# Seven units with seven products, at every second place, in both halves of the second product of two SwiGLU FFNs (fp32, split into high and low parts)

## The chip, the core and the metric

The kernel runs on one core of a Trainium2 chip. The metric is the device time of one execution in microseconds (us). The engines are TensorE (PE; its weight loads are shown apart as PEld), VectorE (DVE), ScalarE (ACT), GpSimd (POOL) and the queues that issue transfers, of which SyncE's (SP) carries the weights.

## The reference

One layer of a hybrid decoder on x of 256 rows and 2048 columns, in float32: a SwiGLU half step, a merge of two gated linear attentions, and a second SwiGLU half step, each with a norm ahead and behind.

```
def rms_norm(x, w):
    y = x * lax.rsqrt(jnp.mean(x * x, axis=-1, keepdims=True) + EPS)
    return y * w

def swiglu(x, w_gate, w_up, w_down):
    return (jax.nn.silu(x @ w_gate) * (x @ w_up)) @ w_down

f1 = swiglu(rms_norm(h, ffn1_pre_norm), ffn1_w_gate, ffn1_w_up, ffn1_w_down)
h = h + 0.5 * rms_norm(f1, ffn1_post_norm)
m = hybrid_token_mixer(rms_norm(h, mix_pre_norm), ...)
h = h + rms_norm(m, mix_post_norm)
f2 = swiglu(rms_norm(h, ffn2_pre_norm), ffn2_w_gate, ffn2_w_up, ffn2_w_down)
h = h + 0.5 * rms_norm(f2, ffn2_post_norm)
```

w_gate and w_up are 2048 x 5504, w_down is 5504 x 2048. The change concerns the product with w_down, once in each FFN.

## The kernel before

Every product of two fp32 matrices is three matmuls of rounded parts: each operand is split into a high part (hi, a copy by ACT to the rounded type fp32r) and a remainder (lo = x - hi, a subtraction by DVE), and PE adds hi by hi, lo by hi and hi by lo into one PSUM tile (mm3, L159 to L161). Each weight that is read from memory costs ACT a copy and DVE a subtraction; the left operand is split too.

The second product of an FFN (down_proj, L589) has 256 rows (two tiles t of 128), 2048 columns in two halves (hf) of two blocks of 512 each, and 5504 summands in 43 tiles kt of 128. Two neighbouring kt make a unit u; there are 21 units and one tile over. A half keeps four sums c in PSUM (two t by two blocks). In the second half, the last seven kt (DTAIL) are held back and done block by block.

- A plain kt loads 128 x 1024 of weights (raw, L135), splits them (whi by ACT at L153, wlo by DVE at L155) and does four products of three matmuls each: 8 products in a unit.
- A unit with seven products (Blocks.seven, L267) treats its 2 x 2 blocks with Strassen's scheme in Winograd's form. It loads four pieces of 128 x 512 into two raw tiles, makes three sums of the weights (wsum, and one in place in raw), splits the four that it needs and the three sums (whi, wlo and wsumh, wsuml), and does 7 products, three into c and four into p, some of them with sums of the left operand (part "d", "s2", "s3", "s4"). Its products p1, p5, p6, p7 collect in four more PSUM tiles (p) over all units of the half. In the order of the code the products are p1, c01, c00, p6, p5, p7, c10; wsuml is needed first by the third matmul of p5.
- share (L306) folds the four p into sums that close adds to the c at the end of the half. Its additions are named psum.
- The sums of the left operand for one unit (sums_of, L762) are four operations of 128 x 128 on DVE (sums, L205 to L208) and a split of 128 x 512. They are made one unit ahead of their first use.

Which units have seven products is set by two tables: DSUMS (3, 7, 11, 15) in both halves, whose operand sums are made in the first half and kept (the first three in the tiles xhi0, xlo0, xhi1, which are free then; they are called held in the profile; the last in a work tile called sums), and DMORE, (9, 19) in the first half and (5, 13) in the second, whose sums are made for the one use in the tiles of the left operand's parts (hkhi, hklo; 4 buffers each).

The left operand's parts of a unit (hkhi by ACT, hklo by DVE, 128 x 512) are made in each half anew from hT. The ring has five buffers each of raw, whi and wlo; the row tiles (wsum, wsumh, wsuml and the sums' first form) have three buffers together.

The code's order is not the engines' order. A scheduler gives each engine a fixed list by priority and by its own idea of when operands are ready; an engine then works through its list in order, waiting where it must. Four loads of the post norm's weights (load_bcast, L384, on ACT's queue) stand at kt 8 to 11 of the first half.

Of the kernel before, what the change touches and what calls it, by code (L numbers as in the profile page):

```python
# [7 lines left out]
F32 = mybir.dt.float32  # L8
F32R = mybir.dt.float32r
# [23 lines left out]
AHEAD = 3  # L33
SUMS = (2, 4, 6)
FOUR = (2, 4, 5, 6)
DSUMS = (3, 7, 11, 15)
DMORE = ((9, 19), (5, 13))
DTAIL = 7
O_GQ, O_GK, O_GV, O_GO, O_CODE = 0, 512, 1024, 2048, 3072
O_HQ, O_HF, O_HI, O_HO, O_ZG, O_ZH = 3088, 4112, 5136, 6160, 7184, 9232  # L40
# [48 lines left out]
def kernel(ctx: ExitStack, tc: tile.TileContext, a: dict, out: bass.AP):  # L89
# [13 lines left out]
    uid, last, first_ops = [0], [None], []  # L103

    def nm(s):
        uid[0] += 1
        return f"{s}_{uid[0]}"
# [276 lines left out]
    def load_bcast(t, name, n, after):  # L384

        with tc.issue_after(after.ins):
            nc.scalar.dma_start(t, a[name][:, n * CB:(n + 1) * CB].broadcast_to([P, CB]))
# [15 lines left out]
    def tiles4(x):  # L403
        return x.rearrange("p (k c) -> p k c", c=P)
# [47 lines left out]
    def square(src, ss, n):  # L452
        sq = work.tile([P, CB], BF16, tag="sq", name=nm("sq"), bufs=1)
        nc.scalar.activation(sq, src, AF.Square, accum_out=ss[:, n:n + 1])  # L454
# [134 lines left out]
    def down_proj(w_dram, nkt, lhs, sums_of, post, pre, wpost, ys, homes, following):  # L589

        acc = [[None] * 4 for _ in range(NT)]
        nxt, rs, ready = ([None] * NT, [None] * NT, [0] * NT), [None, None], []
        ss = [small.tile([P, 4], F32, tag="ss", name=nm("ss")) for _ in range(NT)]
        parts = {}

        def split(hf, kt, alloc=ring_alloc):
            return wchunk(w_dram[kt * P:(kt + 1) * P, hf * 1024:(hf + 1) * 1024]
                          .rearrange("p (n c) -> p n c", n=2), CB, alloc)  # L600

        def weigh(t, n):
            square(acc[t][n], ss[t], n)
            o = acc[t][n]
            if n < 2:
                o = ys()
            elif at_end(t, n):
                o = tmp()

            nc.vector.tensor_tensor(o, acc[t][n], wpost[n], op=ALU.mult)  # L610
            acc[t][n] = o

        def at_end(t, n):
            return pre is None and (t, n) == (NT - 1, 3)

        def tmp():
            return work.tile([P, CB], F32, tag="tmp", name=nm("y"), bufs=3)

        ahead = []
        for hf in range(2):  # L620
            lhs_h = lhs()
            b = Blocks(lambda i, kt: w_dram[kt * P:(kt + 1) * P,
                                            (2 * hf + i) * CB:(2 * hf + i + 1) * CB],
                       CB, lhs_h, part_of(parts))
            n = nkt - DTAIL if hf else nkt
            units = sorted(DSUMS + DMORE[hf])
            kt = 0
            while kt < n:
                u = kt // 2
                if kt % 2 == 0 and u + 1 in units and u + 1 not in parts:  # L630
                    parts[u + 1] = sums_of(u + 1)
                if u in units:
                    b.seven(u, u == units[-1])
                    kt += 2
                    continue
                chunk = ahead.pop(0) if ahead else split(hf, kt)
                if kt == 2 * units[-1] + 2:
                    ahead = [split(hf, kt + 1)]
                    b.share()
                if not hf and kt in (8, 9, 10, 11):  # L640
                    load_bcast(wpost[kt - 8], post, kt - 8, last[0])
                for t in range(NT):
                    for i in range(2):
                        b.plain((kt,), t, i, chunk[i:i + 1], kt == nkt - 1)
                if not hf and kt == 1:
                    side.flush()
                kt += 1
            if not hf:
                ahead = [split(1, kt) for kt in range(2)]
                for t in range(NT):  # L650
                    for i in range(2):
                        acc[t][i] = b.close(t, i)
                        weigh(t, i)
        tail = []
        for i, kt in enumerate(range(nkt - DTAIL, nkt)):
            tail.append((kt, split(1, kt, homes[i])))

            lhs_h(0, kt)
        for t in range(NT):
            for n in (2, 3):  # L660
                for i, (kt, chunk) in enumerate(tail):
                    b.plain((kt,), t, n - 2, chunk[n - 2:n - 1], kt == nkt - 1)
                    if i % 2:
                        side.pump()
                    if following is not None and t == 0 and i == 3 * (n - 2):
                        ready.append(following(len(ready)))

                acc[t][n] = b.close(t, n - 2, tmp() if at_end(t, n) else None)
                weigh(t, n)
                if following is not None and (t, n) == (0, 2):  # L670
                    ready.append(following(len(ready)))
                side.pump()
            side.spawn(settled(t, acc, ss[t], 0.5, pre, nxt, rs))
        return nxt, rs, ready


    def ffn(pre, x, rs, post, pre_next, begin=None, ready=(), then=None):
        with ExitStack() as fctx:
# [4 lines left out]
            def new_part(i):  # L683
                s = ("hkhi", "hklo")[i]
                return fwork.tile([P, 2, NT * P], F32R, tag=s, name=nm(s), bufs=4)
# [34 lines left out]
            for j, f0 in enumerate(blocks):  # L720
# [3 lines left out]
                if j or begin:  # L724
                    g, u, ready = gemm_pair(
                        [(a[pre + "_w_gate"], f0), (a[pre + "_w_up"], f0)], w, xl, sums, ready,
                        following, () if j else raws, (FOUR if j % 2 else SUMS) if j else ())
# [8 lines left out]
                if not (j or begin):  # L736
                    side.spawn(x_sums())
                    u = gemm_block(a[pre + "_w_up"], f0, w, xl)
# [19 lines left out]
            def in_x(s, dt):  # L758
                return tpool.tile([P, 4, CB], dt, tag=s, name=nm("held"))

            wpost = in_x("xlo1", F32)
            def sums_of(u):  # L762
                v = hT[u // 2][:, u % 2 * 2:u % 2 * 2 + 2, :]
                f = row_tile("sums")[:, 0, :]
                four_sums(v[:, 0, :P], v[:, 1, :P], v[:, 0, P:], v[:, 1, P:],
                          *[f[:, k * P:(k + 1) * P] for k in range(4)])
                if any(u in more for more in DMORE):
                    hi, lo = [new_part(i).rearrange("p i c -> p (i c)") for i in range(2)]
                elif u != DSUMS[-1]:
                    home = in_x(("xhi0", "xlo0", "xhi1")[DSUMS.index(u)], F32R)  # L770
                    hi, lo = home[:, 0, :], home[:, 1, :]
                else:
                    hi, lo = [work.tile([P, CB], F32R, tag="tmp", name=nm("sums"), bufs=3)
                              for _ in range(2)]
                split_into(hi, lo, f)
                return tiles4(hi), tiles4(lo)
# [593 lines left out]
```

## Time and profile before

| | |
|---|---|
| time, median of 3 runs | 2064.32 us (2063.22 to 2066.75) |
| the profiled execution's own time | 2066.25 us |
| its span in the profile | 2064.3 us |
| PE busy | 2051.2 us (99%) |
| DVE busy | 1858.0 us (90%) |
| ACT busy | 1304.9 us (63%) |
| DMA, mean over the span | 205 GB/s |

A row of the timeline has the start, the duration, engine, line, operation, what it writes and reads, and its shape; in square brackets stands how long the engine was idle before it and what ended that. A row "PE p L161 <- DVE wsuml L245: 1.8, 3, 0.7" says that PE's matmuls into p of line 161 waited for DVE's wsuml 1.8 us in all, three times, 0.7 at the longest. Matmuls overlap each other, so their durations add up to more than the time that they take. The second products stand at about 462 to 690 us (FFN1) and 1836 to 2058 us (FFN2).

### The profile page before, as it was taken

How to read it: one execution, taken by the hardware profiler on the slowest of the kernel's cores; microseconds unless marked ns; L12 is line 12 of the kernel's file. 1: busy time of each engine (PE TensorE's matmuls, PEld its weight loads, DVE VectorE, ACT ScalarE, POOL GpSimd, SP SyncE). 2: the span in 40 equal slices, each digit the busy share in tenths (PEclk: the TensorE clock that was granted, in tenths of full speed). 3: DMA queues.
4: the chain of work that ended last, by engine and by line, in shares of the span. 5: the costliest groups of instructions: out<-in, count | busy, mean ns of one | idle time of the engine just before them, and what ended most of it. 6: DMA issues, size and time to landing. Idle time of an engine off the chain costs nothing. (4 is left out here: it accounts for less than half of the span.)

```text
span 2064.3 us, 28994 instructions
## 1 busy us (share of the span) xinstructions
PE 2051.2 (99%) x10337; PEld 1702.9 (82%) x10337; DVE 1858.0 (90%) x2187; ACT 1304.9 (63%) x1714; POOL 41.1 (2%) x87
## 2 busy tenths in 40 slices
PE   9999999999999999999999999999999999999998
PEld 9888888888888888878888888888888888888886
DVE  7999999998999779989999897578999999999996
ACT  7666666666666576577655554465666666766663
POOL 1000000000000100000000000010000000000000
PEclk9999999999999999999999999999999999999999
DMA  8767677676767467556565566747767767776663
GB/s 261 215 208 241 196 220 218 209 227 207 226 196 230 148 198 222 162 174 192 169 203 188 181 223 214 218 157 200 234 193 218 227 210 215 219 235 200 213 206 133
DMA packets 246105, 423.50 MB, mean 205 GB/s; under 512 B 63476, under 2 KB 71863, under 8 KB 245960
## 3 DMA queue, kind: packets, MB, share of 16 engines
q1 hardware_dynamic: 194896, 401.80, 61.7%
q10 hardware_dynamic: 51064, 19.84, 4.8%
q8 instruction: 81, 1.33, 0.3%
q14 instruction: 64, 0.52, 0.1%
HBM read 406.11 MB, written 4.19 MB: 199 GB/s over the span
## 5 line engine op out<-in xcount | busy, mean ns | idle before, releaser
L155 DVE TENSOR_TENSOR wlo<-raw,whi 128x1024 fp32r<-128x1024 f32 (+3 forms) x498 | 582.8, 1184 | 70.9 <-ACT whi L153 70.0
L153 ACT ACTIVATE whi<-raw 128x1024 fp32r<-128x1024 f32 (+3 forms) x498 | 504.8, 1026 | 217.5 <-PE c L160 74.0
L159 PE MATMUL c<-whi,xhi 128*128 128x512 f32 (+1 forms) x1270 | 494.5, 390 | 0.0
L161 PE MATMUL c<-wlo,xhi 128*128 128x512 f32 (+1 forms) x1270 | 491.5, 387 | 0.0
L160 PE MATMUL c<-whi,xlo 128*128 128x512 f32 (+1 forms) x1270 | 491.3, 387 | 0.0
L245 DVE TENSOR_TENSOR wlo<-raw,whi 128x1024 fp32r<-128x1024 f32 x252 | 299.4, 1218 | 36.9 <-ACT whi L284 23.6
L161 PEld LDWEIGHTS c<-wlo,xhi 128*128 128x128 f32 x1270 | 238.4, 188 | 47.9 <-DVE wlo L245 0.8
L159 PEld LDWEIGHTS c<-whi,xhi 128*128 128x128 f32 x1270 | 238.4, 188 | 47.4 <-ACT xhi L471 0.6
L160 PEld LDWEIGHTS c<-whi,xlo 128*128 128x128 f32 x1270 | 238.5, 188 | 46.2
L284 ACT ACTIVATE whi<-raw 128x1024 fp32r<-128x1024 f32 x126 | 133.1, 1057 | 201.2 <-DVE raw L245 95.0
L245 DVE TENSOR_TENSOR wsuml<-wsum,wsumh 128x1536 fp32r<-128x1536 f32 x126 | 220.6, 1751 | 8.0 <-ACT wsumh L286 8.0
L160 PE MATMUL c<-whi,hklo 128*128 128x512 f32 x558 | 217.2, 389 | 0.3 <-DVE hklo L155 0.3
L161 PE MATMUL c<-wlo,hkhi 128*128 128x512 f32 x558 | 217.2, 389 | 0.1
L159 PE MATMUL c<-whi,hkhi 128*128 128x512 f32 x558 | 217.2, 389 | 0.0
L282 ACT ACTIVATE wsumh<-wsum 128x1024 fp32r<-128x1024 f32 x126 | 132.6, 1053 | 92.7 <-DVE wsum L245 70.7
L280 ACT ACTIVATE whi<-raw 128x1024 fp32r<-128x1024 f32 x126 | 132.4, 1051 | 60.8 <-PE c L160 49.4
L245 DVE TENSOR_TENSOR wsum<-raw,raw 128x1024 f32<-128x1024 f32 x126 | 153.4, 1218 | 18.2 <-DMA raw<-in_ffn_w_down_dram 15.7
L160 PEld LDWEIGHTS c<-whi,hklo 128*128 128x128 f32 x558 | 104.7, 188 | 22.3 <-DVE hklo L155 0.6
L161 PEld LDWEIGHTS c<-wlo,hkhi 128*128 128x128 f32 x558 | 104.7, 188 | 22.2 <-DVE wlo L245 0.5
L159 PEld LDWEIGHTS c<-whi,hkhi 128*128 128x128 f32 x558 | 104.7, 188 | 21.8
L245 DVE TENSOR_TENSOR c<-c,psum 128x512 f32<-128x512 f32 x135 | 87.4, 690 | 11.5 <-PE c L161 11.2
L245 DVE TENSOR_TENSOR wsum<-raw 128x512 f32<-128x512 f32 x126 | 87.0, 690 | 3.6
(346 smaller groups left out, 3153.4 us busy)
## 6 DMA issues: line engine op xcount, KB each, us to landing
raw<-in_ffn_w_down_dram SPq DMA_DIRECT2D x124, 512.0 KB, 4.7
raw<-in_w_in_dram SPq DMA_DIRECT2D x104, 512.0 KB, 4.5
raw<-in_ffn_w_gate_dram SPq DMA_DIRECT2D x90, 512.0 KB, 4.6
raw<-in_ffn_w_up_dram SPq DMA_DIRECT2D x90, 512.0 KB, 4.4
raw<-in_ffn_w_gate_dram SPq DMA_DIRECT2D x140, 256.0 KB, 4.0
raw<-in_ffn_w_up_dram SPq DMA_DIRECT2D x140, 256.0 KB, 3.9
raw<-in_w_in_dram SPq DMA_DIRECT2D x128, 256.0 KB, 3.6
raw<-in_ffn_w_down_dram SPq DMA_DIRECT2D x96, 256.0 KB, 3.7
```

The source lines that it names most:

```text
L153: last[0] = nc.scalar.activation(hi, src, AF.Copy)
L155: nc.vector.tensor_tensor(lo, src, hi.bitcast(F32), op=ALU.subtract)
L159: nc.tensor.matmul(ps, lhsT=xhi, rhs=whi, start=start, stop=False)
L160: nc.tensor.matmul(ps, lhsT=xlo, rhs=whi, start=False, stop=False)
L161: nc.tensor.matmul(ps, lhsT=xhi, rhs=wlo, start=False, stop=stop)
L245: return nc.vector.tensor_tensor(o, x, y, op=op)
L280: nc.scalar.activation(ahi, ra, AF.Copy)
L282: nc.scalar.activation(hi[:, 0:2, :], wsum[:, 0:2, :], AF.Copy)
L284: nc.scalar.activation(bhi, rb, AF.Copy)
```

## The change

The units with seven products are 3, 5, 7, 9, 11, 13 and 15 in both halves: seven instead of six in each half, 28 instead of 24 in the two second products. Units 9 and 19 of the first half and 5 and 13 of the second were among them before; now 5, 9 and 13 are in both halves, and 19 in none. The operand sums of all seven are made in the first half and kept: two units' sums share each of xhi0, xlo0 and xhi1, of which only half was used before, and the seventh stays in the work tiles. Sums are made 7 times in an FFN, before 8 times (6 in the first half, 2 in the second). Since kt 10 and 11 are now a unit with seven products, two of the four loads of the post norm's weights stand at kt 12 and 13.

```
-DSUMS = (3, 7, 11, 15)
-DMORE = ((9, 19), (5, 13))
+DSUMS = (3, 5, 7, 9, 11, 13, 15)
...
-            units = sorted(DSUMS + DMORE[hf])
+            units = DSUMS
...
-                if not hf and kt in (8, 9, 10, 11):
-                    load_bcast(wpost[kt - 8], post, kt - 8, last[0])
+                if not hf and kt in (8, 9, 12, 13):
+                    col = (8, 9, 12, 13).index(kt)
+                    load_bcast(wpost[col], post, col, last[0])
...
-            wpost = in_x("xlo1", F32)
+            wpost, homes = in_x("xlo1", F32), []
...
-                if any(u in more for more in DMORE):
-                    hi, lo = [new_part(i).rearrange("p i c -> p (i c)") for i in range(2)]
-                elif u != DSUMS[-1]:
-                    home = in_x(("xhi0", "xlo0", "xhi1")[DSUMS.index(u)], F32R)
-                    hi, lo = home[:, 0, :], home[:, 1, :]
+                i = DSUMS.index(u)
+                if i % 2 == 0 and i < 6:
+                    homes.append(in_x(("xhi0", "xlo0", "xhi1")[i // 2], F32R))
+                if i < 6:
+                    hi, lo = [homes[-1][:, 2 * (i % 2) + k, :] for k in range(2)]
                 else:
```

What it makes of the engines' lists lies within the two second products. The first place is DVE's list in the first half of FFN1, from the remainder of unit 3's sums on (wsuml_4254). Before (raw_4302 and raw_4325 are unit 4, raw_4344 and raw_4367 unit 5, raw_4394 the first tile of unit 6):

```order
L245 TENSOR_TENSOR wsuml_4254<-wsum_4252,wsumh_4253 128x1536
L155 TENSOR_TENSOR wlo_4305<-raw_4302,whi_4304 128x1024
L155 TENSOR_TENSOR hklo_4310<-hT_1661,hkhi_4309 128x512
L155 TENSOR_TENSOR wlo_4328<-raw_4325,whi_4327 128x1024
L155 TENSOR_TENSOR wlo_4347<-raw_4344,whi_4346 128x1024
L205 TENSOR_TENSOR sums_4386<-hT_2008 128x128
L155 TENSOR_TENSOR hklo_4352<-hT_1661,hkhi_4351 128x512
L206 SCALAR_TENSOR_TENSOR sums_4386<-sums_4386,hT_2008 128x128
L155 TENSOR_TENSOR wlo_4370<-raw_4367,whi_4369 128x1024
L207 TENSOR_TENSOR sums_4386<-hT_2008 128x128
L208 TENSOR_TENSOR sums_4386<-hT_2008,sums_4386 128x128
L155 TENSOR_TENSOR wlo_4397<-raw_4394,whi_4396 128x1024
```

Now (raw_4309 and raw_4332 are unit 4, wsum_4353 unit 5; sums_4302 and held_4207 are unit 5's operand sums; line numbers are one lower):

```order
L244 TENSOR_TENSOR wsuml_4254<-wsum_4252,wsumh_4253 128x1536
L154 TENSOR_TENSOR wlo_4312<-raw_4309,whi_4311 128x1024
L204 TENSOR_TENSOR sums_4302<-hT_1661 128x128
L206 TENSOR_TENSOR sums_4302<-hT_1661 128x128
L205 SCALAR_TENSOR_TENSOR sums_4302<-sums_4302,hT_1661 128x128
L154 TENSOR_TENSOR hklo_4317<-hT_1661,hkhi_4316 128x512
L207 TENSOR_TENSOR sums_4302<-hT_1661,sums_4302 128x128
L154 TENSOR_TENSOR wlo_4335<-raw_4332,whi_4334 128x1024
L154 TENSOR_TENSOR hklo_4375<-hT_1661,hkhi_4374 128x512
L154 TENSOR_TENSOR held_4207<-sums_4302,held_4207 128x512
L154 TENSOR_TENSOR hklo_4415<-hT_2008,hkhi_4414 128x512
L244 TENSOR_TENSOR wsum_4353<-raw_4351,raw_4352 128x1024
```

Behind unit 3 stood the weights of three plain units; now one plain unit, the next operand sums and the next unit's weight sums stand there.

The second place is DVE's list behind unit 15 of the same half. Before (wlo_4816 is still unit 15, hklo_4859 is the left operand of unit 16, hklo_4899 of unit 17):

```order
L245 TENSOR_TENSOR wsuml_4808<-wsum_4806,wsumh_4807 128x1536
L245 TENSOR_TENSOR wlo_4816<-raw_4805,whi_4815 128x1024
L155 TENSOR_TENSOR hklo_4859<-hT_3767,hkhi_4858 128x512
L205 TENSOR_TENSOR sums_4932<-hT_4102 128x128
L155 TENSOR_TENSOR wlo_4855<-raw_4852,whi_4854 128x1024
```

Now (wsuml_4836 is unit 15's, wlo_4883, wlo_4889 and hklo_4899 are unit 16's, psum is share):

```order
L244 TENSOR_TENSOR wsuml_4836<-wsum_4834,wsumh_4835 128x1536
L154 TENSOR_TENSOR wlo_4883<-raw_4880,whi_4882 128x1024
L154 TENSOR_TENSOR wlo_4889<-raw_4886,whi_4888 128x1024
L244 TENSOR_TENSOR psum_4892<-psum_4892,p_907_4274 128x512
L154 TENSOR_TENSOR hklo_4899<-hT_3767,hkhi_4898 128x512
L244 TENSOR_TENSOR psum_4892<-psum_4892,p_909_4276 128x512
```

Unit 16's left operand moved behind both of its weights and behind the first addition of share, which came after unit 19 before.

The third place is PE's list at the same unit 15, now (p_908 is p5, p_909 is p7, c_865 is c10 of unit 15; the rows with whi_4882, wlo_4883 are unit 16):

```order
L158 MATMUL c_865_4110<-wsumh_4835,hkhi_4855 128x512
L159 MATMUL c_865_4110<-wsumh_4835,hklo_4856 128x512
L158 MATMUL c_863_4108<-whi_4882,hkhi_4898 128x512
L158 MATMUL c_864_4109<-whi_4882,hkhi_4898 128x512
L158 MATMUL c_866_4111<-whi_4882,hkhi_4898 128x512
L160 MATMUL p_908_4275<-wsuml_4836,sums_4788 128x512
L160 MATMUL p_909_4276<-wsuml_4836,sums_4788 128x512
L160 MATMUL c_865_4110<-wsuml_4836,hkhi_4855 128x512
L158 MATMUL c_865_4110<-whi_4882,hkhi_4898 128x512
L159 MATMUL c_863_4108<-whi_4882,hklo_4899 128x512
```

Before, each product's three matmuls stood together here, and unit 16 began behind unit 15's last. Now the matmuls with wsuml stand behind unit 15's other ones and behind three of unit 16's, and the first with hklo_4899 is the fourth behind the first with wsuml_4836.

## The prediction

> **What bounds the kernel now.** I read the page first, then who PE waited for, then tables by stretch, then the rows of PE and DVE in order of time where the change lies.
>
> ```profile
> span 2064.3 us, 28994 instructions
> PE 2051.2 (99%) x10337; PEld 1702.9 (82%) x10337; DVE 1858.0 (90%) x2187; ACT 1304.9 (63%) x1714; POOL 41.1 (2%) x87
> ```
>
> PE is the bound, and DVE at 90% stands close behind it. PE's waits of 2064 us, those on DVE:
>
> ```profile
> PE p L161 <- DVE wsuml L245: 1.8, 3, 0.7
> PE p L161 <- DVE wlo L245: 0.5, 1, 0.5
> PE c L160 <- DVE hklo L155: 0.3, 1, 0.3
> ```
>
> The names are those of the second products: remainders of the weights (wlo), of their sums (wsuml), of the left operand (hklo). The second products by stretch (PE, PEld, DVE, ACT, POOL busy, clock, DMA share, GB/s): the crowded part of FFN1's first half, most of its second half, FFN2's first half.
>
> ```profile
> 475.00:541.00 66.00, 64.67 (x280) 51.95 (x279) 59.87 (x79) 40.36 (x51) 0.00 (x0) 1.00 0.66 206
> 570.00:660.00 90.00, 90.00 (x398) 74.52 (x398) 85.77 (x98) 59.97 (x78) 0.50 (x2) 1.00 0.65 204
> 1834.00:1934.00 100.00, 100.00 (x443) 82.81 (x442) 88.92 (x111) 65.13 (x81) 0.00 (x0) 1.00 0.70 213
> ```
>
> The clock is whole in all three. PE lacks time only in the first, where units 7, 9, 11 follow each other at every second place. Two of its stalls there:
>
> ```profile
> 508.59 0.50 PE L161 MATMUL p<-wsuml,hkhi 128*128 128x512 f32 x1 [0.47 <-DVE wsuml L245]
> 516.86 0.50 PE L161 MATMUL p<-wlo,hkhi 128*128 128x512 f32 x1 [0.49 <-DVE wlo L245]
> ```
>
> So the change adds units of just the kind at which DVE already fell behind.
>
> **What it removes on PE.** Four units in all (two in each FFN) have seven products instead of eight; a product is three matmuls: 12 matmuls less (PE's order has 9022 rows for 9034). Their price, from unit 3 of FFN1's first half (PE, start and duration):
>
> ```profile
> 473.38 0.39 PE L161 MATMUL p<-wlo,hkhi 128*128 128x512 f32 x1
> ...
> 476.10 0.39 PE L161 MATMUL p<-wsuml,held 128*128 128x512 f32 x1
> ```
>
> The second starts 12 matmuls behind the first: 2.72/12 = 0.227 us each. So 12 are worth 2.72 us. The duration of 0.39 overlaps its neighbours. The Trainium skill, "Perfetto Trace Analysis", section "Identifying the Most-Contended Engine", says that matmul busy time is no good measure, as pipelined matmuls look otherwise in the trace. This trace agrees; by the 0.39 the four products would seem worth 4.7 us.
>
> **What it adds on DVE.** A unit's weights cost two subtractions of 128x1024 in the plain form; with seven products they cost three operations of 128x1024, two of 128x512, one of 128x1536. Start to start, where DVE had no idle time:
>
> ```profile
> 505.66 1.22 DVE L155 TENSOR_TENSOR wlo<-raw,whi 128x1024 fp32r<-128x1024 f32 x1
> 506.79 1.75 DVE L245 TENSOR_TENSOR wsuml<-wsum,wsumh 128x1536 fp32r<-128x1536 f32 x1
> 508.46 0.68 DVE L155 TENSOR_TENSOR hklo<-hT,hkhi 128x512 fp32r<-128x512 f32 x1
> 509.06 0.28 DVE L205 TENSOR_TENSOR sums<-hT 128x128 f32<-128x128 f32 x1
> 509.27 0.28 DVE L207 TENSOR_TENSOR sums<-hT 128x128 f32<-128x128 f32 x1
> ...
> 511.79 0.69 DVE L155 TENSOR_TENSOR held<-sums,held 128x512 fp32r<-128x512 f32 x1 [0.70 <-ACT held L153]
> ```
>
> 1.13 us for 1024 columns, 1.67 for 1536, 0.60 for 512, 0.20 for 128. The Trainium skill, "VectorE: DVE Perf Modes", section "The DRAIN you can't avoid", has the next operation start only when the pipe is empty; at whole durations (1.22, 1.75, 0.68, 0.28) each FFN's sum below would be 7.5 us longer and the kernel end near 2085. The trace speaks against it: 505.66 + 1.22 is 506.88, and the next began at 506.79.
>
> A pair of units, one with seven products and one plain, takes PE 45 matmuls: 10.2 us. DVE: five of 1024 (two are the plain unit's), 1536, two of 512, two left operands of 512: 5.65 + 1.67 + 2.40 = 9.7. In a first half the operand sums come on top: four of 128 and one of 512, 1.4 us: 11.1. DVE is 0.9 us too slow for each pair, and there are now six pairs in a row.
>
> **The first half of each FFN.** In the change's DVE order, behind unit 3's wsuml up to and with unit 15's, stand 30 operations of 1024, 30 of 512, 24 of 128 and 6 of 1536: 33.9 + 18.0 + 4.8 + 10.0 = 66.7 us. Up to hklo_4899, unit 16's left operand, come two of 1024 and two of 512 more (one is share's psum): 70.2. PE's first use of that hklo stands 281 matmuls behind unit 3's wsuml matmul, four behind unit 15's: 63.7 us. Up to the first row nothing moves, so both clocks start as before, in FFN1 and in FFN2:
>
> ```profile
> 473.58 1.75 DVE L245 TENSOR_TENSOR wsuml<-wsum,wsumh 128x1536 fp32r<-128x1536 f32 x1
> 475.25 1.22 DVE L155 TENSOR_TENSOR wlo<-raw,whi 128x1024 fp32r<-128x1024 f32 x1
> ...
> 1845.92 1.75 DVE L245 TENSOR_TENSOR wsuml<-wsum,wsumh 128x1536 fp32r<-128x1536 f32 x1
> 1847.59 1.22 DVE L155 TENSOR_TENSOR wlo<-raw,whi 128x1024 fp32r<-128x1024 f32 x1
> ```
>
> and PE's wsuml matmuls of units 3 (476.10 above) and 15, before:
>
> ```profile
> 541.49 0.39 PE L161 MATMUL p<-wsuml,sums 128*128 128x512 f32 x1
> ...
> 1849.57 0.39 PE L161 MATMUL p<-wsuml,held 128*128 128x512 f32 x1
> ...
> 1912.13 0.39 PE L161 MATMUL p<-wsuml,sums 128*128 128x512 f32 x1
> ```
>
> FFN1: hklo is ready at 475.25 + 70.2 + 0.1 = 545.5 (0.1 is the overlap at its end), an unstalled PE wants it at 476.10 + 63.7 = 539.8: a stall of 5.7 in all. FFN2: 1847.59 + 70.3 = 1917.9 against 1849.57 + 63.7 = 1913.3: 4.6. Before, units 3 to 15 were 276 matmuls, 62.6 us: FFN1 took 541.49 - 476.10 = 65.4, a stall of 2.8; FFN2 took 62.6, none. So stalls grow by 10.3 - 2.8 = 7.5.
>
> The psum ahead of hklo waits for PE's p6 and for ACT's copy of p1; both products stand ahead of unit 15's wsuml in PE's order, so they are done by then. Two units' sums now share a kept tile; for both writes the order lists a wait on DVE alone, so unit 5's needn't wait for PE to be done with unit 3's.
>
> That is DVE without idle time. With idle time it is longer: 0.70 us per pair if the sums' remainder waits for ACT as in the last row of the fence on DVE, nothing if the weights' sum that now mostly stands between hides ACT's copy. I take 0.1 per pair, near nothing, since wsum's 1.13 is longer than the 0.70: 1.2 us for 12 pairs. It can't go below nothing.
>
> **What costs nothing, and by what cover.** ACT copies per pair four of 1024, one of 1024 and one of 512 for sums, two left operands and one kept sum:
>
> ```profile
> 505.82 0.62 ACT L153 ACTIVATE hkhi<-hT 128x512 fp32r<-128x512 f32 x1
> 506.34 1.04 ACT L153 ACTIVATE whi<-raw 128x1024 fp32r<-128x1024 f32 x1
> 507.29 1.04 ACT L280 ACTIVATE whi<-raw 128x1024 fp32r<-128x1024 f32 x1
> ```
>
> 5 x 0.95 + 4 x 0.52 = 6.8 us, within 11.1. SP's queue carries 16 transfers of 256 KB in place of 8 of 512; the bytes are the same. One landed and one was missed so:
>
> ```profile
> raw<-in_ffn_w_down_dram SPq DMA_DIRECT2D x96, 256.0 KB, 3.7
> 487.35 1.23 DVE L245 TENSOR_TENSOR wsum<-raw,raw 128x1024 f32<-128x1024 f32 x1 [3.13 <-DMA raw<-in_ffn_w_down_dram]
> ```
>
> A unit's last raw buffer comes free with the first subtraction of the seven before it, 2.8 us ahead of wsuml's end, and is wanted 3.1 behind that: 5.9 for 3.7. Uncovered it could cost up to 3.1 once per FFN. The two moved loads of the post norm's weights (ACT's queue) are wanted only at the half's end. The fifth and thirteenth unit's sums, no longer made twice, and the whole second half lie under PE: pairs there take DVE 9.7 against 10.2, and unit 7 of FFN1's second half, whose pair had no sums to make, kept a lead of 3.2 (609.0 to 612.2):
>
> ```profile
> 607.26 1.75 DVE L245 TENSOR_TENSOR wsuml<-wsum,wsumh 128x1536 fp32r<-128x1536 f32 x1
> 612.21 0.39 PE L161 MATMUL p<-wsuml,held 128*128 128x512 f32 x1
> ```
>
> **The sum.** +7.5 + 1.2 - 2.7 = +6.0 us. The profiled execution took 2066.25, 1.95 more than its span of 2064.3; the median is 2064.32. I carry the difference over: 2070.3.
>
> **The rivals.**
> - Only wsuml decides, and hklo behind it hides. PE's order puts unit 15's wsuml 277 matmuls (62.8 us) behind unit 3's. Then FFN1 is late by 542.0 - 538.9 = 3.1, FFN2 by 1914.4 - 1912.4 = 2.0: 5.1 - 2.8 - 2.7 = -0.4, 2063.9, no change. It decides if DVE comes 2.6 us earlier to this place. For it: 2.6 of 70 us is an error of 4% in the sum. Against: DVE's queue is in order, with 3.5 us of work between wsuml and hklo, where PE has four matmuls. Chance 0.25.
> - Faster: DVE keeps up, and the old stall of 2.8 goes as well: -2.7 - 2.8, 2058.8. It needs a pair at 10.4 us or less instead of 11.1 (10.2, and FFN1's lead of 0.8 or FFN2's of 1.9, from wsuml's end to its matmul, shared over six). Against: the start-to-start rows. Chance 0.05.
> - Each pair idles 0.7 us for ACT, as before: +4.8 + 12 x 0.7 = +13.2, 2077.5. For it: such a gap stood in FFN1's crowded part. Against: wsum stands between in four of six pairs. Chance 0.13.
> - That it doesn't do what it says is excluded by the 12 matmuls.
>
> **How the numbers follow.** The forecast has 0.57. What a measurement here tells from no change is 0.2%, 4.1 us: 2060.2 to 2068.4. Faster 0.05. Same: 0.25, and 0.05 of the forecast where DVE runs without any idle time and a little ahead, 0.30. Slower 0.65. The range goes from just below the no-change rival (2063.5) to just short of the idle one (2076.5).
>
> **What would show it.** In the changed kernel's trace, DVE should be busy without gaps from 475 to 545 and from 1848 to 1918, PE's waits on wlo, wsuml, hklo should be some 10 us and all lie there, the longest before unit 16's hklo; the second halves should show none, and PE's starts elsewhere nothing new. A PE without stalls in the first halves, or a DVE that waits there for raw or for ACT, would prove the sum wrong.

## The result, and the profile after

Before: 2065.92 us (median of 7, 2063.22 to 2067.06). Changed: 2071.78 us (median of 7, 2070.38 to 2073.68). The ratio is 1.003, its 95% interval 1.002 to 1.004: slower by 5.9 us, where 6.0 were forecast. The changed kernel executed again beside the experiments (E7) came out at 2074.93 against 2065.33, 1.0041 (1.0027 to 1.0055), 9.6 us. So the loss lies between some 6 and 10 us, and that the first set met the forecast to 0.1 us is luck.

The page of the changed kernel has 12 matmuls less and 12.6 us more of DVE's work:

```profile
span 2068.6 us, 28999 instructions
PE 2050.2 (99%) x10325; PEld 1699.1 (82%) x10325; DVE 1870.6 (90%) x2193; ACT 1313.8 (64%) x1720; POOL 40.9 (2%) x87
```

The lines on whom PE waited for DVE's remainders (us in all, times, longest), of the whole execution:

```profile
PE c L159 <- DVE hklo L154: 4.6, 3, 2.2
PE p L160 <- DVE wlo L244: 2.6, 3, 1.4
PE p L160 <- DVE wsuml L244: 0.5, 1, 0.5
```

They were 2.6 us together and are 7.7; the left operand's remainder, hklo, stood for 0.3 of them and now stands for 4.6. Not all of it lies in the second products: the 0.5 on wsuml now, and 1.3 of the 1.8 before, stand in FFN2's first product (before at 1435 and 1444 us). In the second products alone PE waited 1.3 us before and 7.2 now, 4.6 on hklo and 2.6 on wlo. (Such a line counts PE as busy up to a matmul's modelled end. Below, a stall is what the time between two starts of PE exceeds 0.227 us, summed over the rows. Matmuls at half clock, see E7, start further apart too, so a stall as it is counted here takes in what they lose.)

By stretch, changed: FFN1's first half from unit 3 to 16, most of its second half, FFN2's first half (PE, PEld, DVE, ACT, POOL busy, clock, DMA share, GB/s):

```profile
475.00:547.00 72.00, 67.54 (x287) 52.59 (x286) 71.97 (x97) 49.03 (x62) 0.00 (x0) 1.00 0.63 197
570.00:660.00 90.00, 90.00 (x399) 74.53 (x398) 86.00 (x92) 59.93 (x76) 0.50 (x2) 1.00 0.64 203
1849.00:1920.00 71.00, 68.18 (x293) 53.95 (x292) 70.97 (x96) 47.84 (x61) 0.00 (x0) 1.00 0.61 199
```

The first and the last stretch before:

```profile
475.00:547.00 72.00, 70.67 (x307) 56.90 (x306) 65.30 (x85) 43.41 (x55) 0.00 (x0) 1.00 0.68 210
1849.00:1920.00 71.00, 71.00 (x315) 58.80 (x314) 63.69 (x84) 41.65 (x53) 0.00 (x0) 1.00 0.69 215
```

The counts in brackets are the thing to read: 72 us hold 317 matmuls at 0.227, and PE got through 287, before through 307. DVE is busy for 71.97 of 72.00 and for 70.97 of 71.00, so it never waited for anything there. The second half has its full 399.

DVE at FFN1's unit 3 and units 15 and 16, and PE at unit 3, at its first long wait (unit 5) and at its two longest (start, duration):

```profile
473.87 1.75 DVE L244 TENSOR_TENSOR wsuml<-wsum,wsumh 128x1536 fp32r<-128x1536 f32 x1
475.54 1.21 DVE L154 TENSOR_TENSOR wlo<-raw,whi 128x1024 fp32r<-128x1024 f32 x1
...
540.99 1.75 DVE L244 TENSOR_TENSOR wsuml<-wsum,wsumh 128x1536 fp32r<-128x1536 f32 x1
542.65 2.35 DVE L154 TENSOR_TENSOR wlo<-raw,whi 128x1024 fp32r<-128x1024 f32 x2
544.92 0.68 DVE L244 TENSOR_TENSOR psum<-psum,p 128x512 f32<-128x512 f32 x1
545.52 0.68 DVE L154 TENSOR_TENSOR hklo<-hT,hkhi 128x512 fp32r<-128x512 f32 x1
546.12 0.68 DVE L244 TENSOR_TENSOR psum<-psum,p 128x512 f32<-128x512 f32 x1
```

```profile
475.67 0.50 PE L160 MATMUL p<-wsuml,held 128*128 128x512 f32 x1
...
485.36 0.50 PE L160 MATMUL p<-wlo,hkhi 128*128 128x512 f32 x1 [1.38 <-DVE wlo L244]
...
543.67 0.39 PE L158 MATMUL c<-whi,hkhi 128*128 128x512 f32 x1
546.26 0.50 PE L159 MATMUL c<-whi,hklo 128*128 128x512 f32 x1 [2.20 <-DVE hklo L154]
...
1918.73 0.50 PE L159 MATMUL c<-whi,hklo 128*128 128x512 f32 x1 [2.18 <-DVE hklo L154]
```

This is the chain that was forecast: unit 15's wsuml, two wlo, the psum of share, hklo, and PE standing in front of it. Stalls in the first halves: 7.2 and 4.7 us, 2.8 and 0 before.

### The profile page after: what moved, and what is told of

Its sections match the earlier page's. It is cut to its first block, busy times and chain, and to the rows that moved or that the text cites. A ratio compares the mean times of both kernels' runs of the same rounds, so it can differ in the third digit from the quotient of the medians.

```text
span 2068.6 us, 28999 instructions
## 1 busy us (share of the span) xinstructions
PE 2050.2 (99%) x10325; PEld 1699.1 (82%) x10325; DVE 1870.6 (90%) x2193; ACT 1313.8 (64%) x1720; POOL 40.9 (2%) x87
## 5 line engine op out<-in xcount | busy, mean ns | idle before, releaser
L154 DVE TENSOR_TENSOR wlo<-raw,whi 128x1024 fp32r<-128x1024 f32 (+3 forms) x490 | 574.6, 1185 | 84.0 <-ACT whi L152 83.5
L152 ACT ACTIVATE whi<-raw 128x1024 fp32r<-128x1024 f32 (+3 forms) x490 | 497.4, 1026 | 226.6 <-PE c L159 79.1
L244 DVE TENSOR_TENSOR wlo<-raw,whi 128x1024 fp32r<-128x1024 f32 x260 | 308.2, 1219 | 34.5 <-ACT whi L283 22.5
L283 ACT ACTIVATE whi<-raw 128x1024 fp32r<-128x1024 f32 x130 | 137.6, 1059 | 202.9 <-DVE raw L244 93.9
L244 DVE TENSOR_TENSOR wsuml<-wsum,wsumh 128x1536 fp32r<-128x1536 f32 x130 | 227.8, 1752 | 8.0 <-ACT wsumh L285 7.6
L159 PE MATMUL c<-whi,hklo 128*128 128x512 f32 x522 | 203.7, 390 | 4.7 <-DVE hklo L154 4.6
L160 PE MATMUL c<-wlo,hkhi 128*128 128x512 f32 x522 | 203.0, 389 | 0.0
L158 PE MATMUL c<-whi,hkhi 128*128 128x512 f32 x522 | 202.3, 389 | 0.0
L279 ACT ACTIVATE whi<-raw 128x1024 fp32r<-128x1024 f32 x130 | 136.7, 1051 | 71.8 <-PE c L159 62.3
L159 PEld LDWEIGHTS c<-whi,hklo 128*128 128x128 f32 x522 | 98.0, 188 | 27.2 <-DVE hklo L154 6.8
L160 PEld LDWEIGHTS c<-wlo,hkhi 128*128 128x128 f32 x522 | 98.0, 188 | 20.6 <-DVE wlo L244 0.3
```

The lines of the kernel that those rows point to most:

```text
L152: last[0] = nc.scalar.activation(hi, src, AF.Copy)
L154: nc.vector.tensor_tensor(lo, src, hi.bitcast(F32), op=ALU.subtract)
L158: nc.tensor.matmul(ps, lhsT=xhi, rhs=whi, start=start, stop=False)
L159: nc.tensor.matmul(ps, lhsT=xlo, rhs=whi, start=False, stop=False)
L160: nc.tensor.matmul(ps, lhsT=xhi, rhs=wlo, start=False, stop=stop)
L244: return nc.vector.tensor_tensor(o, x, y, op=op)
```

## Experiments

The theory: in the first halves DVE's queue is longer than PE's work, because every seven-product unit brings operand sums of 1.4 us and there is one at every second place; the last stall is the order of that queue; the second halves have room. The rivals: only wsuml matters and hklo hides; the loss comes from the second halves; dense units are late by themselves (landing, buffers, ACT), not by the sums.

Each change is against the changed kernel if nothing else is said. "Stalls" are those of FFN1's and FFN2's first half in the profiled execution, then those of both second halves, up to the last matmul of each second product; before has 2.8, 0 and 0.3. In E1, E5 to E8 and E10 they hold matmuls at half clock, 1.7 us or a little less for each stretch of them. "By stalls" is the stalls in all, less before's 3.1, less 0.227 for each matmul saved, worked out before rounding. "Measured" is the median against that of the kernel before, executed beside it.

| kernel | matmuls saved | stalls | by stalls | measured | ratio (95%) |
|---|---|---|---|---|---|
| changed | 12 | 7.2, 4.7, 0.3 | +6.4 | +5.9 | 1.003 (1.002 to 1.004) |
| E1 first halves only | 6 | 7.9, 5.5, 0.3 | +9.2 | +10.6 | 1.0054 (1.0042 to 1.0066) |
| E2 second halves only | 6 | 1.6, 0.2, 0.3 | -2.3 | -2.0 | 0.9995 (0.9987 to 1.0004) |
| E3 one unit's sums | 12 | 0, 0, 0.6 | -5.2 | -5.0 | 0.9977 (0.9968 to 0.9987) |
| E4 left operand first | 12 | 4.7, 2.2, 0.3 | +1.5 | +2.2 | 1.0009 (1.0000 to 1.0017) |
| E5 spread | 12 | 5.9, 2.6, 2.1 | +4.7 | +5.2 | 1.0026 (1.0017 to 1.0036) |
| E6 sums on POOL | 12 | 19.8, 21.4, 0.7 | +36.0 | +35.0 | 1.0167 (1.0153 to 1.0181) |
| E7 changed again | 12 | 8.8, 7.3, 0.7 | +11.0 | +9.6 | 1.0041 (1.0027 to 1.0055) |
| E8 longer stall | 12 | 8.7, 8.0, 0.6 | +11.5 | +11.4 | 1.0052 (1.0039 to 1.0065) |
| E9 spread, left first | 12 | 3.7, 1.7, 0.3 | 0.0 | -0.6 | 0.9996 (0.9987 to 1.0005) |
| E10 spread only | 12 | 4.7, 4.2, 0.3 | +3.4 | +3.6 | 1.0015 (1.0006 to 1.0024) |
| E11 thirteen units | 6 | 0, 0, 0.3 | -4.1 | -4.4 | 0.9978 (0.9969 to 0.9987) |
| E12 fourteen units | 12 | 0.3, 0, 3.5 | -2.1 | -1.7 | 0.9993 (0.9984 to 1.0002) |

Stalls and saved matmuls account for every kernel to about 1 us, but for E1 and E7 (1.4 each). The stalls are those of one execution and the time is a median: E7's profiled execution was the slowest of its five.

**E1, the first halves alone.**

```
-            units = DSUMS
+            units = [u for u in DSUMS if not (hf and u == 9)]
```

> The first halves as in the changed kernel (units 3, 5, ... 15), the second halves as before (unit 9 is plain there again, so 6 matmuls more than the changed kernel). Theory (DVE is too slow for the first halves, the second halves are free): all of the loss stays and the gain of the second halves goes, 2 units x 3 matmuls x 0.227 us = 1.4 us: 2071.8 + 1.4 = 2073.1 us, with PE's stalls in both first halves as in the changed kernel (7.3 and 4.8 us) and none in the second. Rival (the second halves take a share of the loss, through kept sums or buffers): less than 2071.8.

2075.3 us against 2064.66, +10.6: the whole loss is there without the second halves' extra unit, and more than the forecast 2073.1, which was +7.2 against 2065.92. Part of what is beyond it stands in the profile as granted clock. The stretches of 3.4 us around the stall before hklo in FFN1 and the like in FFN2 (the column before the last two is the clock):

```profile
541.90:545.30 3.40, 1.18 (x6) 0.67 (x4) 3.40 (x5) 2.21 (x4) 0.00 (x0) 1.00 0.84 240
545.30:548.70 3.40, 3.38 (x8) 2.71 (x9) 3.40 (x5) 0.89 (x1) 0.00 (x0) 0.50 0.76 263
1917.45:1920.86 3.41, 2.10 (x10) 1.40 (x8) 3.41 (x4) 2.80 (x5) 0.00 (x0) 1.00 0.75 246
1920.86:1924.28 3.42, 2.50 (x11) 2.09 (x12) 3.42 (x5) 1.52 (x2) 0.00 (x0) 1.00 0.77 277
1924.28:1927.70 3.42, 3.42 (x17) 2.84 (x16) 3.42 (x5) 1.88 (x3) 0.00 (x0) 1.00 0.62 184
```

Behind FFN1's stall of 2.4 us PE runs at half clock for 3.4 us, which costs 1.7. FFN2's stall is as long, and isn't followed by it. E7 and E8 take this up.

**E2, the second halves alone**, against the kernel before, whose first halves it keeps (one more kept sum, for unit 9).

```
-            units = sorted(DSUMS + DMORE[hf])
+            units = sorted(DSUMS + DMORE[hf] + ((9,) if hf else ()))
...
+                if u == 9:
+                    hi, lo = [homes[0][:, 2 + k, :] for k in range(2)]
```

> The first halves as before (units 3, 7, 9, 11, 15, 19), the second halves with unit 9 added to the six of before, its sums kept from the first half in a free part of a tile that is held anyway. Theory: a pair of units takes DVE 9.7 us of PE's 10.2 there, so the 6 matmuls less come out whole: 2065.9 - 1.4 = 2064.5 us, no PE stall in the second halves, 2.8 and 0 in the first. Rival (the second halves are pressed too): 2066 or more, with new PE waits on wlo, wsuml or hklo behind unit 7 of a second half.

-2.0 us for a forecast of -1.4; the interval takes in no change, so the time alone settles little, and the first halves, whose units are those of before, had 0.9 us less of stalls in this profile. The second half's row does settle it: DVE 88.4 of 90 us, PE all 90, no waits.

```profile
570.00:660.00 90.00, 90.00 (x399) 74.53 (x398) 88.37 (x101) 59.21 (x78) 0.50 (x2) 1.00 0.63 200
```

With E1: the second halves give their part of the gain, the first halves lose all.

**E3, without the operand sums of units 5 to 15.**

```
-                    parts[u + 1] = sums_of(u + 1)
+                    parts[u + 1] = parts[3] if u + 1 > 3 else sums_of(u + 1)
```

> The changed kernel with the operand sums of units 5 to 15 left out: these units multiply with unit 3's sums (so six units' products are computed with another unit's operand). All matmuls, weights, left operands and loads stay. Theory (the operand sums, 1.4 us of DVE for each pair, make the first halves late): a pair takes DVE 9.7 us against PE's 10.2, the stalls of the first halves go, those of before (2.8) too: 2065.9 - 2.7 - 2.8 = 2060.4 us, 2059.5 to 2062. Rival (seven units close to each other are late by themselves, through the landing of their weights, the buffers or ACT, and the sums lie in idle time): stalls of 5 us or more stay, 2066 to 2071.8.

2059.65 us. The same two stretches as in the changed kernel:

```profile
475.00:547.00 72.00, 72.00 (x320) 59.61 (x319) 71.44 (x75) 46.44 (x59) 0.00 (x0) 1.00 0.71 230
1849.00:1920.00 71.00, 71.00 (x315) 58.76 (x315) 67.94 (x70) 46.33 (x58) 0.00 (x0) 1.00 0.71 228
```

320 matmuls instead of 287, with the same units at the same places, the same weights and loads. The rival that dense units are late by themselves falls: it is the 1.4 us of sums to a pair. (ACT's copies of these sums go too, but it was DVE that had no idle time.)

**E4, the left operand first.**

```
+                if not hf and kt == 2 * units[-1] + 2:
+                    lhs_h(0, kt)
...
-                if kt == 2 * units[-1] + 2:
+                if kt == 2 * units[-1] + (2 if hf else 6):
                     ahead = [split(hf, kt + 1)]
                     b.share()
```

> The changed kernel with unit 16's left operand split ahead of unit 16's weights in the first halves, and share made two units later there. DVE does the same work, in another order. Theory (the last stall of each first half, 2.5 us before unit 16's hklo in either FFN, is DVE's queue: 3.5 us of work between unit 15's wsuml and that hklo, where PE has four matmuls): both stalls go, and only wsuml decides: 2071.8 - 4.9 = 2066.9 us, 2066 to 2068. Rival (DVE is late by what it has to do in all, so that a moved operand only moves the wait to the next wlo, hklo or psum): 2070 to 2072.

2066.81 us, 2066.9 forecast; against the kernel before, +2.2 for a forecast of +1.0 (2066.9 against 2065.92). DVE now goes from wsuml straight to hklo, and the waits on hklo are gone but for 0.2 (the rows are of the whole execution; those on wsuml lie in FFN2's first product):

```profile
541.74 1.74 DVE L244 TENSOR_TENSOR wsuml<-wsum,wsumh 128x1536 fp32r<-128x1536 f32 x1
543.41 0.67 DVE L154 TENSOR_TENSOR hklo<-hT,hkhi 128x512 fp32r<-128x512 f32 x1
544.01 3.48 DVE L154 TENSOR_TENSOR wlo<-raw,whi 128x1024 fp32r<-128x1024 f32 x3
```

```profile
PE p L160 <- DVE wlo L244: 2.5, 3, 1.4
...
PE p L160 <- DVE wsuml L244: 0.9, 2, 0.6
...
PE c L159 <- DVE hklo L154: 0.2, 1, 0.2
```

The same work in another order is 5.0 us cheaper in stalls (7.2 + 4.7 less 4.7 + 2.2). That is the whole of what the prediction put behind unit 15's wsuml.

**E7, the changed kernel again, and E8, a longer stall.** E8:

```
-                    ahead = [split(hf, kt + 1)]
+                    ahead = [split(hf, kt + 1 + i) for i in range(1 if hf else 2)]
```

> The changed kernel again, beside the others of this call. Ledger theory: 12.1 us of PE stalls in the first halves against 2.8 before, 12 matmuls less: +6.6 us, 1.003 of before. Second theory, from the first run of E1: a stall of 2.4 us can be followed by 3.4 us at half the granted clock, 1.7 us more each time, in some executions. Then executions with a mean clock of 0.998 are about 1.7 us, and with 0.997 about 3.4 us longer than those with 0.999, and the kernel before has 0.999 nearly always. Rival: clock and span are unrelated, or before shows the same spread.

> The changed kernel with one more chunk of weights (1.13 us of DVE) split ahead of unit 16's left operand in each first half: the stall of 2.4 us before that operand is 3.5. Nothing else is added: the chunk is split earlier, not twice. Ledger theory alone: +1.1 us in each FFN, 2.3 us above the changed kernel of this call. With the clock theory (a stall of this length brings 3.4 us of half clock): both FFNs have it in nearly every execution, mean clock 0.997, and another 1 to 2 us on top, since it already came in part of the changed kernel's executions: 3 to 4.5 us above it. Rival (the half clock has nothing to do with the stall): clock as in the changed kernel, 2.3 us.

E7's profile shows both FFNs' stalls followed by half clock, in stretches of 3.4 us (before, during and behind it in FFN1; before and during in FFN2):

```profile
545.40:548.80 3.40, 1.43 (x6) 1.21 (x7) 3.40 (x5) 2.53 (x3) 0.00 (x0) 1.00 0.82 258
548.80:552.20 3.40, 3.40 (x9) 2.67 (x9) 3.40 (x5) 1.06 (x1) 0.00 (x0) 0.50 0.78 272
552.20:555.60 3.40, 3.40 (x16) 2.76 (x16) 3.40 (x4) 1.58 (x2) 0.00 (x0) 0.99 0.73 220
1921.00:1924.40 3.40, 1.19 (x5) 0.66 (x5) 3.40 (x5) 2.29 (x4) 0.00 (x0) 1.00 0.81 240
1924.40:1927.80 3.40, 3.40 (x9) 2.66 (x9) 3.40 (x5) 1.11 (x2) 0.00 (x0) 0.50 0.80 276
```

The stretch at half clock has 9 matmuls, the next one 16: nothing waits, PE is simply slower. E7's +9.6 us lie 3.0 above the +6.6 that the ledger alone gave. Over the twelve executions of the changed kernel the mean clock is 0.999 in two, 0.998 in six, 0.997 in four, with medians of 2072.1, 2071.5 and 2074.4 us; the kernel before, executed beside E1 to E8, has 0.999 in 36 of 40 and 0.998 in four. A mean of 0.998 alone says little, since three of E11's eleven executions have it too, and its profile has no stall in the first halves; 0.997 does not occur in the kernel before. The groups overlap, so the forecast of 1.7 us a step is borne out by the profiles, not by the spread of these times. (E1's six executions do come in the clock's order: 2072.0 at 0.999, 2074.7 to 2075.6 at 0.998, 2077.2 and 2077.7 at 0.997.)

E8's stalls before hklo are 3.5 us, and both FFNs have the half clock behind them. It took 1.8 us more than E7, by the ledger 2.3, by the clock theory as I put it 3 to 4.5. So its time is nearer to the rival, and one of its five executions has 0.999 in spite of the longer stall: that the half clock follows the stall is seen in the profiles, not in E8's time. As E7 had the half clock nearly as often, there was little left to add; that number of mine was wrong.

**E5, E9 and E10: as many units, further apart.** E5's edit (E9 and E10 have 3, 6, 9, 11, 13, 15, 18 in the first halves and the changed kernel's in the second):

```
-DSUMS = (3, 5, 7, 9, 11, 13, 15)
+DSUMS = (3, 5, 7, 9, 12, 14, 16)
+DFIRST = (3, 6, 9, 12, 14, 16, 19)
+DMORE = {4: 5, 7: 7}
...
-            units = DSUMS
+            units = DSUMS if hf else DFIRST
...
+                if not hf and kt % 2 == 0 and u in DMORE:
+                    parts[DMORE[u]] = sums_of(DMORE[u])
```

> As many seven-product units as the changed kernel, elsewhere: first halves 3, 6, 9, 12, 14, 16, 19, second halves 3, 5, 7, 9, 12, 14, 16; unit 19's successor has its left operand split first. Units 5's and 7's sums are made in the first half too and kept, so the first half makes nine sums, two more than the changed kernel. Theory (DVE against PE over the whole stretch decides): from unit 3 to 19 DVE has 6 x 6.3 for the weights of seven-product units, 10 x 2.3 for plain ones, 16 x 0.6 left operands and 8 x 1.4 sums, 81 us, PE 366 matmuls, 83: no stall to speak of, in either half. The stalls of before (2.8) go, and 12 matmuls: 5.5 us below before, 0.9973 of it; stalls of 1 us in FFN1 at most. Rival (seven-product units in such number are late wherever they stand): within 0.1% of before or slower, with stalls of 5 us or more.

A miss: 1.0026 instead of 0.9973. In the longest stalls PE waits for a copy by ACT, not for one of DVE's remainders. E10 shows the same place, ACT and then PE:

```profile
479.26 1.05 ACT L281 ACTIVATE whi<-raw 128x1024 fp32r<-128x1024 f32 x1
483.58 1.06 ACT L283 ACTIVATE wsumh<-wsum 128x1024 fp32r<-128x1024 f32 x1 [3.27 <-DVE wsum L246]
484.55 0.61 ACT L154 ACTIVATE hkhi<-sums 128x512 fp32r<-128x512 f32 x1
485.07 0.61 ACT L154 ACTIVATE hkhi<-hT 128x512 fp32r<-128x512 f32 x1
```

```profile
485.73 2.03 PE L160 MATMUL c<-whi,hkhi 128*128 128x512 f32 x4 [2.63 <-ACT hkhi L154]
```

ACT stood idle for 3.27 us before unit 6's wsumh, until DVE's queue had come to unit 6's wsum, with the copy of unit 5's left operand queued two behind it. The order had been made with unit 6's sums ahead of unit 5's left operand. So DVE's queue has a part in it, by way of ACT's.

> E9 without the left operands first: only the places of the units differ from E5. If ACT's order is the cause of E5's stalls, they are back: 5.8 us in all, 1.000 of before, with some executions at half clock behind the stall of 2.8. If the number of sums or units is the cause in E5, E10 and E9 have the same time.

> Fourteen seven-product units in each FFN as in the changed kernel: first halves 3, 6, 9, 11, 13, 15, 18, second halves 3, 5, 7, 9, 11, 13, 15; units 5's and 7's sums made in the first half too and kept; and in the first halves each unit's left operand is split ahead of its weights and of the next unit's sums. E5 had DVE 5 us and more ahead of PE for the weights, and stalls only where ACT's copy of unit 5's left operand stood behind unit 6's sums in ACT's queue (2.8 + 0.7 us in FFN1, 1.7 + 0.7 in FFN2), and at the last of the second half (1.4), where its last seven-product unit was 16. Ledger theory: with those gone no stall is left in the second products, 12 matmuls and before's 2.8 us are saved: 5.5 us below before, 0.9973. Rival (nine sums and seven such units are more than DVE or ACT can hold in a first half, the stalls move elsewhere): 0.9995 to 1.002 of before.

E9 adds, over E10, what E4 did, for every unit:

```
+                if not hf and u >= 3:
+                    lhs_h(0, kt)
```

E10 has E5's stalls back at unit 5 and both half clocks, 1.0015; E9 has none on ACT or hklo, and is 4.2 us quicker. But E9 kept 3.7 and 1.7 us of stalls, nearly all on wlo at units 11, 13 and 15, where four units stand at every second place again: part of my expectation, that they would go too, failed.

**E6, the sums on POOL** (with E4's edit).

```
-                four_sums(v[:, 0, :P], v[:, 1, :P], v[:, 0, P:], v[:, 1, P:],
...
+                tt = nc.gpsimd.tensor_tensor
+                tt(d, a22, a21, op=ALU.subtract)
+                tt(s3, a11, a21, op=ALU.subtract)
+                tt(s4, a21, a22, op=ALU.subtract)
+                tt(s2, s4, a11, op=ALU.subtract)
+                tt(s4, a12, s2, op=ALU.add)
```

> E4 (left operand first) with the four additions of each unit's operand sums on POOL, as five operations there, in place of four on DVE; their split into hi and lo stays on ACT and DVE. Theory (DVE's time decides): 0.8 us less on DVE for each unit with sums, a pair 10.3 against PE's 10.2, so E4's stalls (4.9 and 2.3) shrink by up to 4.8 in each FFN to 1 us or less: 5 us below before, 0.9975 of it. Rival 1 (POOL is slow at them or takes DVE's access to memory, so that DVE's operations beside them grow longer or wait for the sums): the stalls stay, 1.001 of before or slower. POOL's time for such an operation is not in the trace of before; PE uses a unit's sums about 5 us behind the place where they are issued.

35 us slower: the rival. (Six stretches of 3.4 us at half clock in its profile, see E7, are some 10 us of it.) POOL's operations for one unit, and DVE beside them:

```profile
489.89 2.45 POOL L770 TENSOR_TENSOR sums<-hT 128x128 f32<-128x128 f32 x1 [9.14 <-DVE wsuml L244]
492.31 0.45 POOL L771 TENSOR_TENSOR sums<-hT 128x128 f32<-128x128 f32 x1
492.72 0.45 POOL L772 TENSOR_TENSOR sums<-hT 128x128 f32<-128x128 f32 x1
493.26 0.46 POOL L773 TENSOR_TENSOR sums<-sums,hT 128x128 f32<-128x128 f32 x1
493.80 0.46 POOL L774 TENSOR_TENSOR sums<-hT,sums 128x128 f32<-128x128 f32 x1
```

```profile
489.67 2.35 DVE L154 TENSOR_TENSOR wlo<-raw,whi 128x1024 fp32r<-128x1024 f32 x2
494.95 0.70 DVE L154 TENSOR_TENSOR held<-sums,held 128x512 fp32r<-128x512 f32 x1 [2.93 <-ACT held L152]
```

The sums begin only when DVE is done with wsuml (the releaser in the first row), take 4.4 us instead of 0.8, and ACT (whose next copy is theirs) and DVE behind it stand still: DVE for 2.93 us here, more than the 0.8 that it was spared. The first POOL operation ends 0.3 us behind DVE's two subtractions, 2.45 us for what takes 0.45 alone. The Trainium skill, "SBUF — State Buffer", section "Who interferes with whom", says that a DVE instruction with two operands in SBUF and a GpSimd instruction that reads SBUF shut each other out for a whole instruction; this trace agrees (2.45 against 0.45).

**E11 and E12: what the ledger allows.** E9's kernel with the sums of second-half units moved out of the crowded part (E12: first halves 3, 6, 9, 12, 15, 17, 19, and only unit 5's sums, at 20):

```
+DFIRST = (3, 6, 9, 12, 15, 18)
+KEPT = (3, 9, 5, 7, 11, 13)
+DMORE = {19: 5, 20: 7}
...
```

> Thirteen seven-product units in each FFN, one less than the changed kernel: first halves 3, 6, 9, 12, 15, 18 (never at every second place), second halves 3, 5, 7, 9, 11, 13, 15. In the first half the left operands are split first, as in E9; the sums of units 5 and 7 are made behind the last such unit, at 19 and 20, those of 11 and 13 in the second half; all these are kept. Ledger theory: from unit 3 to 18 DVE has 5 x 6.3 + 10 x 2.3 + 15 x 0.6 + 5 x 1.4 = 70 us, PE 345 matmuls, 78: no stall in a first half, before's 2.8 gone, and 6 matmuls less than before, 1.4: 4.2 us below before, 0.998. Rival (E9's stalls of 3.8 and 1.8 us come from the left operands put first, not from the pairs and the early sums): stalls of over 2 us remain, 0.9990 or more.

> As many seven-product units as the changed kernel, with E11's rules: first halves 3, 6, 9, 12, 15, 17, 19, second halves 3, 5, ... 15; unit 5's sums made at unit 20, those of 7, 11, 13 in the second half. Ledger theory: DVE from unit 3 to 19 has 6 x 6.3 + 10 x 2.3 + 16 x 0.6 + 6 x 1.4 = 78 us, PE 366 matmuls, 83; second half 6 x 9.7 + 3 x 1.4 = 62.4 against 61.2 with 3.2 of lead: no stall, 12 matmuls (2.7) and 2.8 of stalls saved: 5.5 us below before, 0.9973. Rival (two pairs at the end of a first half, or three sums in the second, are too many): stalls of 2 us or more there, 0.9985 or more.

E11: 2060.82 us, 0.9978, as forecast (0.998), and quicker than both kernels. PE is busy for all of both stretches, and neither first half has a stall.

```profile
475.00:560.00 85.00, 85.00 (x377) 70.41 (x376) 83.16 (x111) 55.92 (x70) 0.00 (x0) 1.00 0.69 222
570.00:660.00 90.00, 90.00 (x399) 74.55 (x398) 88.79 (x101) 60.84 (x78) 0.50 (x2) 1.00 0.62 200
```

E12 has next to no stalls in its first halves either, as forecast, but 3.5 us in its second halves, where three units' sums are made, and the kernel stays at 0.9993:

```profile
570.00:660.00 90.00, 89.12 (x390) 72.48 (x389) 89.85 (x107) 60.53 (x80) 0.39 (x2) 1.00 0.62 201
```

DVE 89.85 of 90: the second half is now what the first was. My 62.4 against 61.2 with 3.2 of lead was right on the shortage and wrong on the lead: FFN1's second half begins with a wait of 0.29 us on hklo, at 574.58, so DVE comes late out of the first half, which ends with two such units close to each other. Which of the two weighs more, these units or the third unit's sums, wasn't separated.

## Why the prediction was right

- **The saved matmuls.** 12 fewer on the page, 2.7 us, and E2's second halves kept theirs. The sentence of the Trainium skill that the prediction names here ("Perfetto Trace Analysis", section "Identifying the Most-Contended Engine") has pipelined matmuls look smaller in a trace; here a row looks longer, 0.39 us for a pace of 0.227, so the trace agrees with the advice and not with its reason.
- **DVE's ledger.** Forecast from unit 3's wsuml to the end of unit 16's hklo: 70.2 us. Measured 475.54 to 546.12, where the next operation starts: 70.6; FFN2 1848.00 to 1918.59: 70.6. The start-to-start prices held to 0.6%. The rule that the prediction sets against these prices is only half of what the Trainium skill says in "VectorE: DVE Perf Modes", section "The DRAIN you can't avoid": the same section adds that a next operation that is not held starts earlier. The prediction's rows agree with that (a start at 506.79, where the one before ended at 506.88).
- **The stalls.** From unit 3's wsuml to unit 16's hklo, FFN1: 5.7 forecast, 6.7 measured; FFN2: 4.6 and 4.5 (7.2 and 4.7 in the whole halves). FFN1's miss is the step "Up to the first row nothing moves, so both clocks start as before". The order is the same up to there, but unit 3's wsuml (473.87 + 1.75) ended 0.05 us ahead of its matmul, not 0.77: DVE came 0.3 later and PE 0.4 earlier. In FFN2 this lead was 2.30, where 1.90 was carried over; that it made up there for 0.4 us more of DVE's work is luck.
- **What DVE lacks, and the lead.** Stall and lead together are 6.8 us in both FFNs of the changed kernel, of E7 and of E1 (leads 0.05 and 2.30; 0.06 and 1.27; 0.66 and 1.46), where the forecast has 6.5. So what DVE lacks is the same each time, and how much of it PE feels goes by the lead at unit 3. The three have the same lists up to there, so the lead differs between executions and not by the edit; why wasn't tried.
- **Idle time of DVE.** 1.2 us allowed, 0.03 in either stretch: the term should have been nothing. It made up by luck for most of FFN1's miss: 7.5 + 1.2 = 8.7 forecast, 7.2 + 4.7 - 2.8 = 9.1 measured.
- **hklo behind two wlo and share.** Right, and E4 prices it: 5.0 us, 5.2 by the prediction's own two sums (5.7 - 3.1 and 4.6 - 2.0). The rival that only wsuml decides (2063.9) needed hklo hidden; PE stood 2.4 us before it in either FFN.
- **The other rivals.** DVE keeping up: E3's world, not this one. A gap of 0.7 us for ACT in each pair: none, DVE is busy throughout.
- **The covers.** PE and DVE waited for no copy by ACT, raw or moved load in the first halves from unit 3 to 16; the second halves have no waits.
- **A misread view.** The prediction puts all of PE's waits on wsuml, wlo and hklo into the second products; 1.3 of the 2.6 us lie in FFN2's first product (1435 and 1444 us). No term of its sum rests on that: the 2.8 us of old stalls came from PE's starts.
- **What was missing.** The clock. The profiled execution has a whole clock: stalls and matmuls give +6.4, and its span grew by 4.3 only because the rest was shorter than in the profile of before, by 0.4 us ahead of unit 3 of FFN1 and by 1.5 between the two second products' crowded parts (unit 16 of FFN1 to unit 3 of FFN2). In E7's profile the two half clocks cost 3.4 us on top. That the median came out at +5.9 and not above in the first set, and at +9.6 in the second, isn't settled beyond this. Nor did the forecast's 2070.3 itself hold: it starts from 2064.32, the median of three; with four more executions before's median is 2065.92, and the changed kernel's 2071.78 lies 1.5 above the forecast.

## What to carry to other kernels

Where PE is the bound and DVE at 90%, an edit that saves PE time and costs DVE time is to be summed by stretch, with DVE's start-to-start times, up to the last operand that PE wants there. What stands in the queue between the last late operand and the next one wanted counts as well: E4 moved one operand ahead of two subtractions and of share, and got 5.0 of the 9.1 us back. Where half of the saving (E11, 6 matmuls) is spread so that DVE has room in each stretch, it comes out whole, and the old stalls go with it.

## What the runs showed of the hardware that I had not expected

- **A stall of 2.4 us can halve the clock.** In the profiles of E1, E5 to E8 and E10 the granted clock falls to 0.50 for 3.4 us (once, in E6, for 6.8) after stalls of 2.3 to 3.5 us before a single operand; 1.7 us for each 3.4. As a rule it follows where PE stood idle for about 2 us or more of one stretch of 3.4 us (E7: busy 1.43 and 1.19 of 3.40), and the stretches keep step over a kernel: E7's half clocks begin at 548.8 and 1924.4, 403 times 3.413 apart. E1's second stall fell across two stretches (busy 2.10 and 2.50) and had none. Both long stalls in the changed kernel's first profile fell so too (2.16 and 2.44, 2.45 and 2.17), and its clock is whole. The line isn't sharp: in E5 a half clock followed a stretch with 1.73 busy, in E6 none followed stretches with 1.51 and 1.73. No stall of 1.9 us or less was followed by it. The Trainium skill, "TensorE: Matmul & The Clock Gate", section "What's actually happening", has a free-running window of 3413 ns, which agrees; its section "HAM oscillation — how this bites in real kernels" warns of gaps above some 3.4 us, and here 2.4 were enough.
- **POOL beside DVE.** An operation of 128x128 took 0.45 us alone and up to 2.45 beside DVE's subtractions, and two of these took up to 2.62 together in place of 2.35 (E6).
